# Gated feed-forward input projections from tile 5 on: one 512-column matmul over both parts of the residual in place of two of 256, with a second read-out and a written order on four engines

## The chip, the cores and the metric

The kernel runs on one core of a Trainium2 chip. The core has five engines that run side by side and meet only through semaphores: TensorE (PE in the rows below, with its weight loads shown apart as PEld), VectorE (DVE), ScalarE (ACT), GpSimd (POOL) and SyncE (SP), which here only issues transfers. TensorE reads both operands from SBUF and writes into PSUM, which has eight banks of 512 fp32 columns per partition. The metric is the device time of one execution in microseconds, the median of the runs.

## What is computed

A decoder trunk of two layers over 256 positions and 1,024 features, all in fp32: in each layer an attention block and then a gated feed-forward block with a short causal convolution. The change lies in the feed-forward block, which runs twice (D_FF is 2,816):

```python
def rmsnorm(x, g):
    y = xf * lax.rsqrt(jnp.mean(xf * xf, axis=-1, keepdims=True) + EPS)
    return (y * g.astype(jnp.float32)).astype(x.dtype)
...
def conv_ffn(h, w_in, conv_w, conv_b, w_out):
    u, g = jnp.split(h @ w_in, 2, axis=-1)
    g = lax.conv_general_dilated(g, conv_w[:, None, :], window_strides=(1,),
                                 padding=[(CONV_WIDTH - 1, 0)], ...
                                 feature_group_count=D_FF) + conv_b
    return (jax.nn.gelu(g, approximate=False) * u) @ w_out
...
    h = h + conv_ffn(rmsnorm(h, ffn_norm[layer]), ffn_w_in[layer], ...)
```

## The kernel before

**Two-part operands.** To keep fp32 accuracy with matmuls on a rounded type, each operand is held as a rounded part and the exact rest: weights as `whi` and `wlo`, the residual (times its norm gain, transposed, features on the partitions) as `xh` and `xl`, the activations of the feed-forward block as the two halves of a tile `o`. A product is three matmuls: high by high, high by rest, rest by high. `xh` and `xl` are each eight blocks (`KD`) of 128 features by 256 positions.

**Weights.** `PLAN` lists the weights in chunks of 128 x 2,048 in the order of use. SP loads a chunk into `raw` (three buffers), ACT copies it to `whi` (L144), DVE subtracts to get `wlo` (L145), each in two pieces of 1,024 columns; there are four buffer pairs. `need(name)` loads up to three chunks ahead and splits up to two ahead.

**A feed-forward tile.** The block runs over 22 tiles `f` of 128 of the 2,816 inner features. `dense(f)` multiplies all 256 positions with the tile's two weight blocks, u and g, into the two halves of one PSUM bank `pd`: 2 x 8 x 3 = 48 matmuls of 256 columns, by `colmajor`. `gate(f)` then multiplies the bank by the norm factor into `gbuf` (DVE, L743), runs the convolution (ACT L749, DVE L751 and L752), gelu (ACT L754), the product with u (POOL L755) and the split into `o` (ACT L757, DVE L758). Four tiles later (`LAGF`) `proj(f)` adds the tile's part of the output projection to accumulators `acc`, which keep their banks for the whole block: four banks and 24 matmuls of 256 columns for each tile in the first layer; five banks and 15 matmuls (nine of 512 columns, six of 256) in the second, whose output comes out positions first. In the second layer four sets of transposes (`phn`) bring the residual into that form; they stand behind tiles 6 to 9.

**Order.** TensorE takes its instructions in the order in which the program writes them. The order on the other engines is found by a scheduler, except at the start of the program. After tile 21, `proj` runs for the four tiles left over; in the second layer bank by bank (`TAIL`), for each bank tiles 18 to 21, and each finished bank is normalised and stored while the next one is summed.

Of the kernel before, what the change touches and what calls it, by code (L numbers as in the profile page):

```python
# [21 lines left out]
F32 = mybir.dt.float32  # L22
F32R = mybir.dt.float32r
AF = mybir.ActivationFunctionType
ALU = mybir.AluOpType
# [22 lines left out]
FIRST = 4  # L48
POOLSHARE = 3
TAIL = ((0, 0, 512), (0, 512, 1024), (1, 0, 512), (1, 512, 768), (1, 768, 1024))  # L50

# [49 lines left out]
def trunk(ctx, tc, x, rel_bias, small, lam_p, wpack, fin_g, onehot, addrow, tab, out):  # L101
# [21 lines left out]
    def pair(a):  # L123
        return a.rearrange("p (a b) -> p a b", a=2)

# [1 line left out]
    chunks, raws, splits = {}, {}, {}  # L127
# [44 lines left out]

# [1 line left out]
    iot = consts.tile([128, 128], F32)  # L174
# [8 lines left out]
    sel = consts.tile([128, 128], F32)  # L183
# [1 line left out]
    scr = consts.tile([128, 1], F32)  # L185
# [17 lines left out]

# [1 line left out]
    xh = xpool.tile([128, KD, S], F32R, name="xh")  # L205
    xl = xpool.tile([128, KD, S], F32R, name="xl")
    sqs = {}
# [57 lines left out]

# [1 line left out]
    def passmajor(items, ks):  # L267
# [23 lines left out]

# [1 line left out]
    Tt = consts.tile([128, 12, S], F32)  # L293
# [17 lines left out]

# [1 line left out]
    BLK = ((0, 256), (256, 384))  # L313
# [136 lines left out]

# [1 line left out]
    def proj_tile(acc, o, w, kk, first, last):  # L452
# [15 lines left out]

# [1 line left out]
    def interleave(env, units, tasks, store, first=0):  # L470
# [19 lines left out]
    def bc2(t):  # L490
        return t[:, None, :].to_broadcast([128, 2, S])
# [239 lines left out]

# [1 line left out]
    gbuf = [consts.tile([128, 2, S + 2], F32, name=f"gbuf{i}") for i in range(3)]  # L733
# [3 lines left out]
    def ffn(l, final):  # L737
        env, acts, box = {}, {}, {}
        cc = ccol[l]

        def gate(f, p):
            gb = gbuf[f % 3]
            nc.vector.tensor_tensor(gb[:, :, 2:], pair(p), bc2(env['r_bc']), op=ALU.mult)  # L743
            u, g = gb[:, 0], gb[:, 1]

            def col(i):
                return cc[:, i * NF + f:i * NF + f + 1]
            t1 = work.tile([128, S], F32, name="t1", tag="sc")
            nc.scalar.activation(t1, g[:, 2:], AF.Identity, bias=col(3), scale=col(2))  # L749
            t3 = work.tile([128, S], F32, name="t3", tag="pt", bufs=6)  # L750
            nc.vector.scalar_tensor_tensor(t3, g[:, 1:S + 1], col(1), t1, op0=ALU.mult, op1=ALU.add)  # L751
            nc.vector.scalar_tensor_tensor(t3, g[:, 0:S], col(0), t3, op0=ALU.mult, op1=ALU.add)  # L752
            ge = work.tile([128, S], F32, name="ge", tag="ex", bufs=6)
            nc.scalar.activation(ge, t3, AF.Gelu)  # L754
            nc.gpsimd.tensor_tensor(ge, ge, u[:, 2:], op=ALU.mult)  # L755
            o = t2("o", F32R)
            nc.scalar.activation(o[:, 0], ge, AF.Copy)  # L757
            nc.vector.tensor_tensor(o[:, 1], ge, o[:, 0].bitcast(F32), op=ALU.subtract)  # L758
            acts[f] = (o[:, 0], o[:, 1])

        def ug_items(p, f):
# [4 lines left out]
        def dense(f):  # L766
            p = bank("pd")
            colmajor(ug_items(p, f))
            gate(f, p)

        def proj(f):
            w = need(f"f{l}o{f // 2}")
            first, last = f == 0, f == NF - 1
            if first:
                box['acc'] = [bank("acc") for _ in range(len(TAIL) if final else 4)]
            if not final:
                proj_tile(box['acc'], acts[f], w, f % 2, first, last)
                return
            for i in range(len(TAIL)):
                proj_tail(f, i)  # L780

        def proj_tail(f, i):
            w = need(f"f{l}o{f // 2}")
            (oh, ol), (hi, lo) = acts[f], w
            tb, c0, c1 = TAIL[i]
            a = box['acc'][i][:, :c1 - c0]
            s = slice(tb * 128, (tb + 1) * 128)
            mm(a, oh[:, s], hi[:, f % 2, c0:c1], f == 0, False)
            mm(a, ol[:, s], hi[:, f % 2, c0:c1], False, False)
            mm(a, oh[:, s], lo[:, f % 2, c0:c1], False, f == NF - 1)  # L790
# [15 lines left out]
        hn = []  # L806
        for f in range(3, NF):
            dense(f)
            if f >= LAGF:
                proj(f - LAGF)  # L810
            if final and f >= 6 and len(hn) < 4:
                i = len(hn)
                p = bank("phn")
                for k in range(4):
                    kk = (i % 2) * 4 + k
                    nc.tensor.transpose(p[:, k * 128:(k + 1) * 128],
                                        hT[:, kk, (i // 2) * 128:(i // 2 + 1) * 128], ident)
                t = t2("hn", shape=(128, 512))
                nc.scalar.activation(t, p, AF.Copy)
                hn.append(t)  # L820
        if not final:
# [36 lines left out]

    # =================== program ===================
    warm = bank("warm")  # L860
# [114 lines left out]
```

## Time and profile before

| | us |
|---|---|
| median of 3 runs (lowest, highest) | 610.53 (610.17, 610.88) |
| profiled execution, first to last instruction (span) | 608.3 |
| TensorE busy in the span | 594.7 |
| VectorE, ScalarE, GpSimd busy | 410.6, 332.3, 116.0 |

The 2.2 us between the median and the span lie outside the first and last instruction of the profile. A matmul is pipelined: a row gives its own length, which overlaps the next one; the pace of a stretch is its length divided by its number of matmuls. Busy time of the other engines is an average over stages; whether an engine is late in a stage is seen from who waits there.

### The profile page before, as it was taken

The numbers are of one execution on the slowest core, as the hardware profiler recorded it, in microseconds if no ns is written. First come the engines' busy times: TensorE is split into PE (matmuls) and PEld (weight loads), VectorE is DVE, ScalarE is ACT, GpSimd is POOL, SyncE is SP. The second block draws the span as 40 slices with busy tenths as digits, with TensorE's granted clock in tenths as the row PEclk, the third lists the DMA queues.
The fourth block names the chain that finished last, engine by engine and source line by source line (L and its number), as shares of the span: only waits on it lengthen the run. The fifth ranks groups of instructions, "written<-read, shape, count | busy, mean of one in ns | idle before, by whom it ended". The sixth has DMA issues, their size and how long they took to land.

```text
span 608.3 us, 11226 instructions
## 1 busy us (share of the span) xinstructions
PE 594.7 (98%) x4622; PEld 571.0 (94%) x4622; DVE 410.6 (67%) x710; ACT 332.3 (55%) x579; POOL 116.0 (19%) x97
## 2 busy tenths in 40 slices
PE   8898999999999999999999999999999999999995
PEld 7887989999999999999999998999999999999994
DVE  5688767679765566656677884658976557665644
ACT  6458557566554445554564664646655445554433
POOL 4701022041201111111153111004120111111100
PEclk9999999999999999999999999999999999999998
DMA  8998544435545554554435333344554554455201
GB/s 278 334 333 297 201 152 142 154 124 208 185 167 204 208 201 157 197 204 156 159 141 208 138 140 140 139 157 155 208 197 155 204 208 175 173 206 184 94 2 70
DMA packets 19964, 108.83 MB, mean 179 GB/s; under 512 B 2430, under 2 KB 5448, under 8 KB 7752
## 3 DMA queue, kind: packets, MB, share of 16 engines
q1 hardware_dynamic: 16416, 104.17, 46.4%
q10 hardware_dynamic: 3336, 3.41, 1.8%
q8 instruction: 36, 0.59, 0.4%
q0 software_dynamic: 160, 0.52, 0.3%
q14 instruction: 16, 0.13, 0.1%
HBM read 107.02 MB, written 1.08 MB: 178 GB/s over the span
## 4 chain that ended last, share of the span: by engine, by line
PE 88%; DMA 4%; DVE 4%; issue 1%; ACT 1%; POOL 1%; SPq 0%; POOLq 0%; DVEq 0%; ACTq 0%
PE pd L121 50%; PE acc L121 27%; DMA raw<-in_wpack_dram 4%; PE pv L121 4%; DVE wlo L145 2%; PE pO L121 2%; PE pS L121 2%; PE puq L121 1%; DVE ex L340 1%; DVE sc L330 1%; PE pukv L121 0%; PE pT L344 0%; ACT whi L144 0%; ACT sqt L218 0%; PE pss L121 0%
## 5 line engine op out<-in xcount | busy, mean ns | idle before, releaser
L144 ACT ACTIVATE whi<-raw 128x1024 fp32r<-128x1024 f32 (+1 forms) x195 | 196.9, 1035 | 131.0 <-PE pd L121 70.3
L121 PE MATMUL pd<-xh,whi 128*128 128x256 f32 x928 | 260.7, 286 | 1.6 <-ACT whi L144 1.3
L121 PE MATMUL pd<-xh,wlo 128*128 128x256 f32 x928 | 258.0, 283 | 0.4 <-DVE wlo L145 0.4
L121 PE MATMUL pd<-xl,whi 128*128 128x256 f32 x928 | 257.8, 283 | 0.0
L145 DVE TENSOR_TENSOR wlo<-raw,whi 128x1024 fp32r<-128x1024 f32 (+1 forms) x183 | 222.5, 1234 | 36.4 <-ACT whi L144 36.2
L121 PEld LDWEIGHTS pd<-xh,whi 128*128 128x128 f32 x928 | 175.6, 191 | 3.4 <-ACT whi L144 1.7
L121 PEld LDWEIGHTS pd<-xh,wlo 128*128 128x128 f32 x928 | 175.7, 192 | 0.8 <-DVE wlo L145 0.8
L121 PEld LDWEIGHTS pd<-xl,whi 128*128 128x128 f32 x928 | 175.7, 192 | 0.1
L121 PE MATMUL acc<-o,whi 128*128 128x256 f32 x608 | 108.7, 280 | 0.0
L755 POOL TENSOR_TENSOR ge<-ge,gbuf 128x256 f32<-128x256 f32 x44 | 50.1, 1141 | 285.2 <-ACT ge L754 285.2
L121 PEld LDWEIGHTS acc<-o,whi 128*128 128x128 f32 x608 | 93.1, 188 | 0.3 <-issue 0.2
L121 PE MATMUL acc<-o,wlo 128*128 128x256 f32 x304 | 85.2, 280 | 0.0
L743 DVE TENSOR_TENSOR gbuf<-pd,r_bc 128x512 f32<-128x512 f32 x44 | 30.0, 690 | 50.7 <-PE pd L121 50.7
L121 PE MATMUL acc<-whi,o 128*128 128x512 f32 (+1 forms) x220 | 57.8, 349 | 0.0
L121 PEld LDWEIGHTS acc<-o,wlo 128*128 128x128 f32 x304 | 57.1, 188 | 0.0
L758 DVE TENSOR_TENSOR o<-ge,o 128x256 fp32r<-128x256 f32 x44 | 19.2, 444 | 49.9 <-ACT o L757 49.9
L757 ACT ACTIVATE o<-ge 128x256 fp32r<-128x256 f32 x44 | 18.4, 418 | 50.9 <-POOL ge L755 50.9
L145 POOL TENSOR_TENSOR wlo<-raw,whi 128x1024 fp32r<-128x1024 f32 (+1 forms) x12 | 26.5, 2206 | 102.6 <-ACT whi L144 56.0
L121 PEld LDWEIGHTS acc<-whi,o 128*128 128x128 f32 x220 | 38.2, 188 | 5.8
L121 PE MATMUL acc<-wlo,o 128*128 128x512 f32 (+1 forms) x110 | 38.3, 348 | 0.0
L754 ACT ACTIVATE ge<-t 128x256 f32<-128x256 f32 x44 | 17.8, 410 | 34.8 <-DVE t L752 34.8
L333 ACT ACTIVATE ex<-sc,nm 128x256 f32<-128x256 f32 (+1 forms) x56 | 24.8, 445 | 10.1 <-DVE nm L330 8.3
(153 smaller groups left out, 553.6 us busy)
## 6 DMA issues: line engine op xcount, KB each, us to landing
raw<-in_wpack_dram SPq DMA_DIRECT2D x95, 1024.0 KB, 4.8
raw<-in_wpack_dram SPq DMA_DIRECT2D x8, 256.0 KB, 4.5
Tt<-btab ACTq DMA_DIRECT2D x2, 1024.0 KB, 9.9
hT<-in_x_dram SPq DMA_DIRECT2D x4, 256.0 KB, 4.8
Tt<-btab ACTq DMA_DIRECT2D x1, 512.0 KB
raw<-in_wpack_dram SPq DMA_DIRECT2D x1, 512.0 KB
fin<-in_fin_g_dram POOLq DMA_DIRECT2D x2, 256.0 KB, 3.7
out_dram<-y SPq DMA_DIRECT2D x2, 256.0 KB, 3.1
```

Source lines behind the costliest of these rows:

```text
L121: nc.tensor.matmul(o, l, r, start=start, stop=stop, skip_group_check=True)
L144: nc.scalar.activation(hi[:, s], raw[:, s], AF.Copy)
L145: (eng or nc.vector).tensor_tensor(lo[:, s], raw[:, s], hi[:, s].bitcast(F32), op=ALU.subtract)
L330: nc.vector.tensor_tensor_reduce(out=t[:, a:b], in0=p[:, a:b], in1=rev(T, b - a), scale=-1.0, scalar=BIG, op0=ALU.add, op1=ALU.min, accum_ ...
L333: nc.scalar.activation(e[:, a:b], t[:, a:b], AF.Exp, bias=nm[:, i:i + 1], scale=-1.0, accum_out=den[:, i:i + 1])
L340: nc.vector.tensor_scalar(e[:, a:b], e[:, a:b], rd[:, i:i + 1], None, op0=ALU.mult)
L743: nc.vector.tensor_tensor(gb[:, :, 2:], pair(p), bc2(env['r_bc']), op=ALU.mult)
L754: nc.scalar.activation(ge, t3, AF.Gelu)
L755: nc.gpsimd.tensor_tensor(ge, ge, u[:, 2:], op=ALU.mult)
L757: nc.scalar.activation(o[:, 0], ge, AF.Copy)
L758: nc.vector.tensor_tensor(o[:, 1], ge, o[:, 0].bitcast(F32), op=ALU.subtract)
```

## The change

`xh` and `xl` become the two halves of each block of one tile `xs`, so that the 512 columns of a block's both parts lie side by side. Tiles 0 to 4 are as before. From tile 5 (`NARROW`) to 21, in both layers, u and g get a PSUM bank each. In each block a matmul of 512 columns takes `whi` over both parts of the residual, its two results standing in the two halves of the bank, and one of 256 columns adds `wlo` times the high part to the lower half. The halves must then be added: ACT copies the upper half to SBUF (`lowp`), DVE adds the lower half to it (`ug`), for u and g, and the product with the norm factor reads `ug`. In these tiles the orders of ACT, DVE, POOL and SP are those of the program text too, with the weight splits placed by hand among the steps of the gate; gelu and the split of tile f-1 stand inside tile f. The transposes of the second layer move to tiles 3 and 4, two sets each.

```diff
-    xh = xpool.tile([128, KD, S], F32R, name="xh")
-    xl = xpool.tile([128, KD, S], F32R, name="xl")
+    xs = xpool.tile([128, KD, 2, S], F32R, name="xs")
+    xh, xl = xs[:, :, 0], xs[:, :, 1]
...
+        def weights(f):
+            n = f"f{l}o{f // 2}"
+            return need(n) if f < NARROW - LAGF or f >= NF - LAGF else chunks[n]
+
         def proj(f):
-            w = need(f"f{l}o{f // 2}")
+            w = weights(f)
...
-        for f in range(3, NF):
+        for f in range(3, NARROW):
             dense(f)
+            if final:
+                hn_tile()
+                hn_tile()
             if f >= LAGF:
                 proj(f - LAGF)
-            if final and f >= 6 and len(hn) < 4:
...
+        def next_chunk():
+            i = split_at[0]
+            if i >= len(PLAN):
+                return [lambda: None] * 2
+            split_at[0] += 1
+            ps = pieces(i)[1]
+
+            def step(n):
+                if n == 0:
+                    open_split(i)
+                if n < len(ps):
+                    split_piece(i, ps[n])
+                if n == 1:
+                    load_next()
+            return [lambda: step(0), lambda: step(1)]
+
+        def product(f, i, p):
+            hi, lo = chunks[f"f{l}i{f}"]
+            for k in range(KD):
+                mm(p, hi[:, 8 * i + k], xs[:, k], k == 0, False)
+                mm(p[:, :S], lo[:, 8 * i + k], xs[:, k, 0], False, k == KD - 1)
+
+        def read_out(t, i, p):
+            lowp = work.tile([128, S], F32, name="lowp", tag="ex", bufs=6)
+            nc.scalar.activation(lowp, p[:, S:], AF.Copy)
+            nc.vector.tensor_tensor(t[:, i], p[:, :S], lowp, op=ALU.add)
+
+        need(f"f{l}i{NARROW}")
+        with tc.manual_schedule(engines={mybir.EngineType.Activation, mybir.EngineType.DVE,
+                                         mybir.EngineType.Pool, mybir.EngineType.SP}):
+            t3 = None
+            for f in range(NARROW, NF):
+                even = f % 2 == 0
+                pu, pg = bank("pd"), bank("pd")
+                product(f, 0, pu)
+                product(f, 1, pg)
+                if even:
+                    c = next_chunk()
+                    c[0]()
+                if t3 is not None:
+                    ge = gelu(f - 1, t3)
+                if even:
+                    c[1]()
+                if t3 is not None:
+                    act_split(f - 1, ge)
+                ug = t2("ug")
+                read_out(ug, 0, pu)
+                read_out(ug, 1, pg)
+                nc.vector.tensor_tensor(gbuf[f % 3][:, :, 2:], ug, bc2(env['r_bc']), op=ALU.mult)
+                c = next_chunk()
+                c[0]()
+                t3 = taps(f, conv(f))
+                c[1]()
+                proj(f - LAGF)
+            act_split(NF - 1, gelu(NF - 1, t3))
```

`conv`, `taps`, `gelu` and `act_split` are the steps of the former `gate`, cut apart and otherwise as they were.

On TensorE, in the first layer, the end of one tile's projection and the start of the next tile before:

```order
L121 MATMUL acc<-o,wlo 128x256
L121 MATMUL pd<-xh,whi 128x256
L121 MATMUL pd<-xl,whi 128x256
L121 MATMUL pd<-xh,wlo 128x256
L121 MATMUL pd<-xh,whi 128x256
L121 MATMUL pd<-xl,whi 128x256
L121 MATMUL pd<-xh,wlo 128x256
```

and the same kind of place now:

```order
L122 MATMUL pd<-xs,whi 128x512
L122 MATMUL pd<-xs,wlo 128x256
L122 MATMUL pd<-xs,whi 128x512
L122 MATMUL pd<-xs,wlo 128x256
L122 MATMUL pd<-xs,whi 128x512
```

Each pair of matmuls with the same `whi` block has become one of 512 columns, so 48 instructions for a tile are 32; the columns are as many as before.

On VectorE, one even and one odd tile in the middle of the first layer before (`t_` is the convolution):

```order
L743 TENSOR_TENSOR gbuf_125<-pd,r_bc 128x2x256
L145 TENSOR_TENSOR wlo<-raw,whi 128x1024
L751 SCALAR_TENSOR_TENSOR t_2571<-gbuf_125,ccol_309,t_2569 128x256
L145 TENSOR_TENSOR wlo<-raw,whi 128x1024
L752 SCALAR_TENSOR_TENSOR t_2571<-gbuf_125,ccol_309,t_2571 128x256
L145 TENSOR_TENSOR wlo<-raw,whi 128x1024 x2
L758 TENSOR_TENSOR o<-ge,o 128x256
L743 TENSOR_TENSOR gbuf_123<-pd,r_bc 128x2x256
```

and now, from the last step of an odd tile over an even one to the read-out of the next:

```order
L146 TENSOR_TENSOR wlo<-raw,whi 128x1024 x3
L767 TENSOR_TENSOR o<-ge,o 128x256
L877 TENSOR_TENSOR ug<-pd,lowp 128x256 x2
L900 TENSOR_TENSOR gbuf_122<-ug,r_bc 128x2x256
L146 TENSOR_TENSOR wlo<-raw,whi 128x1024
L754 SCALAR_TENSOR_TENSOR t_2617<-gbuf_122,ccol_308,t_2615 128x256
L755 SCALAR_TENSOR_TENSOR t_2617<-gbuf_122,ccol_308,t_2617 128x256
L146 TENSOR_TENSOR wlo<-raw,whi 128x1024
L767 TENSOR_TENSOR o<-ge,o 128x256
L877 TENSOR_TENSOR ug<-pd,lowp 128x256 x2
```

The read-out of a tile stands behind two weight splits and the activation split of the tile before in even tiles, and behind the activation split alone in odd ones.

On ScalarE, the last two tiles of the second layer before (`fsq` belongs to the final norm):

```order
L749 ACTIVATE t_6674<-gbuf_125,ccol_310 128x256
L144 ACTIVATE whi<-raw 128x1024
L754 ACTIVATE ge<-t_6676 128x256
L757 ACTIVATE o<-ge 128x256
L749 ACTIVATE t_6764<-gbuf_123,ccol_310 128x256
L754 ACTIVATE ge<-t_6766 128x256
L757 ACTIVATE o<-ge 128x256
L839 ACTIVATE fsq,fss_6794<-hn 128x512 x2
```

and now:

```order
L748 ACTIVATE t_6426<-gbuf_124,ccol_309 128x256
L145 ACTIVATE whi<-raw 128x1024
L760 ACTIVATE ge<-t_6428 128x256
L766 ACTIVATE o<-ge 128x256
L876 ACTIVATE lowp<-pd 128x256 x2
L748 ACTIVATE t_6496<-gbuf_122,ccol_309 128x256
L760 ACTIVATE ge<-t_6498 128x256
L766 ACTIVATE o<-ge 128x256
L925 ACTIVATE fsq,fss_6527<-hn 128x512 x2
```

Two copies have come between the last product and the last tile's gate.

## Rows read from the trace of the kernel before

**Rows 1.** The page: span, and busy time of each engine with its instructions.

```profile
span 608.3 us, 11226 instructions
PE 594.7 (98%) x4622; PEld 571.0 (94%) x4622; DVE 410.6 (67%) x710; ACT 332.3 (55%) x579; POOL 116.0 (19%) x97
```

**Rows 2.** The page: chain that ended last, share of span by line.

```profile
PE pd L121 50%; PE acc L121 27%; DMA raw<-in_wpack_dram 4%; PE pv L121 4%; DVE wlo L145 2%; PE pO L121 2%; PE pS L121 2%; PE puq L121 1%; DVE ex L340 1%; DVE sc L330 1%; PE pukv L121 0%; PE pT L344 0%; ACT whi L144 0%; ACT sqt L218 0%; PE pss L121 0%
```

**Rows 3.** Busy us by engine, tiles 7 to 21, layer one; then clock, DMA share.

```profile
171.69:297.65 125.96, 125.96 (x1058) 125.96 (x1058) 77.48 (x101) 60.89 (x87) 17.16 (x15) 1.00 0.50 184
```

**Rows 4.** Waits of PE in the whole span, from the longest: total, times, longest.

```profile
PE pT L344 <- DVE rd L335: 1.4, 1, 1.4
PE pd L121 <- ACT whi L144: 1.3, 2, 0.7
```

**Rows 5.** The chain in order of time: start, length, what, number of instructions.

```profile
82.70 5.47 PE pv L121 x24
...
151.68 2.83 PE acc L121 x24
154.51 5.75 PE pd L121 x48
...
297.65 14.14 PE acc L121 x120
...
501.79 2.79 PE acc L121 x15
...
587.19 8.40 PE acc L121 x39
```

**Rows 6.** Groups by line and shape: busy us, mean ns, idle before, releaser.

```profile
L144 ACT ACTIVATE whi<-raw 128x1024 fp32r<-128x1024 f32 x187 | 191.8, 1052 | 129.5 <-PE pd L121 70.3 <-issue 22.7 <-PE acc L121 17.8
L145 DVE TENSOR_TENSOR wlo<-raw,whi 128x1024 fp32r<-128x1024 f32 x179 | 219.7, 1246 | 36.3 <-ACT whi L144 36.2
L743 DVE TENSOR_TENSOR gbuf<-pd,r_bc 128x512 f32<-128x512 f32 x44 | 30.0, 690 | 50.7 <-PE pd L121 50.7
L749 ACT ACTIVATE t<-gbuf,ccol 128x256 f32<-128x256 f32 x44 | 25.9, 590 | 5.4 <-DVE gbuf L743 5.4
L752 DVE SCALAR_TENSOR_TENSOR t<-gbuf,ccol,t 128x256 f32<-128x256 f32 x44 | 21.7, 497 | 0.1
L751 DVE SCALAR_TENSOR_TENSOR t<-gbuf,ccol,t 128x256 f32<-128x256 f32 x44 | 20.9, 479 | 0.7 <-ACT t L749 0.7
L758 DVE TENSOR_TENSOR o<-ge,o 128x256 fp32r<-128x256 f32 x44 | 19.2, 444 | 49.9 <-ACT o L757 49.9
L757 ACT ACTIVATE o<-ge 128x256 fp32r<-128x256 f32 x44 | 18.4, 418 | 50.9 <-POOL ge L755 50.9
L754 ACT ACTIVATE ge<-t 128x256 f32<-128x256 f32 x44 | 17.8, 410 | 34.8 <-DVE t L752 34.8
L360 DVE TENSOR_TENSOR o<-pO,o 128x256 fp32r<-128x256 f32 x12 | 4.9, 420 | 7.7 <-ACT o L359 7.7
L359 ACT ACTIVATE o<-pO 128x256 fp32r<-128x256 f32 x12 | 4.5, 385 | 6.3 <-PE pO L121 6.3
```

**Rows 7.** The page: issues of weight loads, KB each, us to landing.

```profile
raw<-in_wpack_dram SPq DMA_DIRECT2D x95, 1024.0 KB, 4.8
```

**Rows 8.** Timeline of tiles 19 and 21 in the second layer, by engine.

```profile
575.28 1.81 POOL L755 TENSOR_TENSOR ge<-ge,gbuf 128x256 f32<-128x256 f32 x1 [8.26 <-ACT ge L754]
590.25 0.64 POOL L755 TENSOR_TENSOR ge<-ge,gbuf 128x256 f32<-128x256 f32 x1 [6.15 <-ACT ge L754]
...
587.23 0.69 DVE L743 TENSOR_TENSOR gbuf<-pd,r_bc 128x512 f32<-128x512 f32 x1 [2.22 <-PE pd L121]
...
591.38 0.42 DVE L758 TENSOR_TENSOR o<-ge,o 128x256 fp32r<-128x256 f32 x1 [1.72 <-ACT o L757]
...
590.93 0.42 ACT L757 ACTIVATE o<-ge 128x256 fp32r<-128x256 f32 x1 [0.82 <-POOL ge L755]
...
591.92 0.63 PE L121 MATMUL acc<-whi,o 128*128 128x512 f32 x2
```

More of the change, by code (lines that the diff above doesn't have):

```diff
@@ L49 @@
 POOLSHARE = 3
+NARROW = 5
 TAIL = ((0, 0, 512), (0, 512, 1024), (1, 0, 512), (1, 512, 768), (1, 768, 1024))
@@ L739, in ffn, with col, conv, taps @@
         cc = ccol[l]
[L741 to L747, printed above, removed]
+        def col(f, i):
+            return cc[:, i * NF + f:i * NF + f + 1]
+        def conv(f):
+            g = gbuf[f % 3][:, 1]
             t1 = work.tile([128, S], F32, name="t1", tag="sc")
-            nc.scalar.activation(t1, g[:, 2:], AF.Identity, bias=col(3), scale=col(2))
+            nc.scalar.activation(t1, g[:, 2:], AF.Identity, bias=col(f, 3), scale=col(f, 2))
+            return t1
+        def taps(f, t1):
+            g = gbuf[f % 3][:, 1]
             t3 = work.tile([128, S], F32, name="t3", tag="pt", bufs=6)
-            nc.vector.scalar_tensor_tensor(t3, g[:, 1:S + 1], col(1), t1, op0=ALU.mult, op1=ALU.add)
-            nc.vector.scalar_tensor_tensor(t3, g[:, 0:S], col(0), t3, op0=ALU.mult, op1=ALU.add)
+            nc.vector.scalar_tensor_tensor(t3, g[:, 1:S + 1], col(f, 1), t1, op0=ALU.mult, op1=ALU.add)
+            nc.vector.scalar_tensor_tensor(t3, g[:, 0:S], col(f, 0), t3, op0=ALU.mult, op1=ALU.add)
+            return t3
+        def gelu(f, t3):
             ge = work.tile([128, S], F32, name="ge", tag="ex", bufs=6)
             nc.scalar.activation(ge, t3, AF.Gelu)
-            nc.gpsimd.tensor_tensor(ge, ge, u[:, 2:], op=ALU.mult)
+            nc.gpsimd.tensor_tensor(ge, ge, gbuf[f % 3][:, 0, 2:], op=ALU.mult)
+            return ge
+        def act_split(f, ge):
             o = t2("o", F32R)
@@ L759, in gate @@
             acts[f] = (o[:, 0], o[:, 1])
+        def gate(f, p):
+            nc.vector.tensor_tensor(gbuf[f % 3][:, :, 2:], pair(p), bc2(env['r_bc']), op=ALU.mult)
+            act_split(f, gelu(f, taps(f, conv(f))))
         def ug_items(p, f):
@@ L782, in proj_tail @@
         def proj_tail(f, i):
-            w = need(f"f{l}o{f // 2}")
+            w = weights(f)
             (oh, ol), (hi, lo) = acts[f], w
@@ L806, in ffn, with hn_tile @@
         hn = []
-        for f in range(3, NF):
+        def hn_tile():
+            i = len(hn)
+            p = bank("phn")
+            for k in range(4):
+                kk = (i % 2) * 4 + k
+                nc.tensor.transpose(p[:, k * 128:(k + 1) * 128],
+                                    hT[:, kk, (i // 2) * 128:(i // 2 + 1) * 128], ident)
+            t = t2("hn", shape=(128, 512))
+            nc.scalar.activation(t, p, AF.Copy)
+            hn.append(t)
+        for f in range(3, NARROW):
@@ L808, in ffn, with load_next @@
             dense(f)
+            if final:
+                hn_tile()
+                hn_tile()
             if f >= LAGF:
                 proj(f - LAGF)
-            if final and f >= 6 and len(hn) < 4:
[L812 to L820, printed above, removed]
+        def load_next():
+            while raw_at[0] < min(split_at[0] + 3, len(PLAN)):
+                load_raw(raw_at[0])
+                raw_at[0] += 1
```

## The prediction

> **What bounds the kernel now.** The page comes first: TensorE is busy for 594.7 of 608.3 us, and no other engine for more than 410.6 [rows 1]. Busy time alone proves little, since it is a mean over stages, so the chain that ended last is next: half of it is the matmuls into `pd`, another 27% those into `acc` [rows 2]. Both together are the feed-forward blocks and some projections. Then the stage itself, by windows: from tile 7 to tile 21 of the first layer TensorE works for 125.96 of 125.96 us at full clock, VectorE for 77.48, ScalarE for 60.89, GpSimd for 17.16, the transfers half of the time [rows 3]. In the whole span TensorE's two longest waits are 1.4 and 1.3 us, and the one of `pd` (1.3 us in two waits) is all that an end to such waits could return there [rows 4]. So in the changed tiles nothing is waited for: the time of a tile is the time of its matmuls, and what the change is worth is read from their pace.
>
> In order of time the chain shows the pace. A tile's input product takes 5.75 us for 48 matmuls of 256 columns, 119.8 ns each. The first layer's `proj` takes 2.83 us for 24, 117.9 ns each. For 512 columns there are two stages: `pv` of the attention, 5.47 us for 24, 227.9 ns each, and the second layer's `proj`, 2.79 us for nine of 512 and six of 256; with 117.9 ns for the six, 231.4 ns remain for each of the nine [rows 5]. A matmul of 512 columns costs less than two of 256 in all of them, though only by 4 to 12 ns.
>
> **The matmuls: the term that carries the sum.** A tile had 48 matmuls of 256 columns, 12,288 columns; it gets 16 of 512 and 16 of 256, the same 12,288. What is saved is therefore only what a matmul costs beyond its columns, for 16 instructions a tile, and there are 17 tiles (5 to 21) in each of two layers, 34 in all, 544 pairs. No row has a residual block of 512 columns as the moving operand, so the cost is bounded from the nearest rows:
> - cheap end: 227.9 and 117.9 ns, 16 times their sum is 5.533 us a tile, 0.217 less than 5.75, 7.4 us over 34 tiles;
> - dear end: 231.4 and 119.8 ns, 5.619 us, 0.131 less, 4.4 us.
>
> I take the middle, 229.7 and 118.9 ns, 5.576 us a tile, 0.174 less: 5.9 us. Neither end is nearer: `pv` is a stage of 512 columns alone, the second layer's `proj` mixes both widths as the new tiles do, but with the activations as the stationary operand. A gain of nothing is not excluded; it is the first rival.
>
> **The read-out and the written order: hidden work.** Added to each tile are two copies of 128 x 256 out of PSUM on ScalarE (0.385 us each by `o<-pO`) and two adds from PSUM on VectorE (0.420 us by `o<-pO,o`); the product with the norm factor stays at 0.69 us [rows 6]. That is 0.77 us on ScalarE and 0.84 on VectorE, beside matmuls. Does it fit? An odd tile splits one weight chunk, an even one two. VectorE in an even tile: four pieces at 1.246, the activation split 0.444, two adds 0.84, the product 0.69, two convolution steps 0.976, in all 7.93 us; in an odd one, with two pieces, 5.44. A tile now lasts 5.58 + 2.83 = 8.41 us, a pair 16.8, against 13.4 us of VectorE. ScalarE has 6.40 and 4.29 us, from the same rows. The pair fits, the even tile narrowly.
>
> Since the orders are fixed, I laid one pair out by hand with these durations. In an even tile that begins at 0, VectorE ends the odd tile's last split at 2.2, the next two splits at 4.7, the activation split at 5.1, and frees the u bank at 5.5 and the g bank at 6.4. The first layer has four banks beside the accumulators, the second three; there the next tile's g product takes the freed u bank, at 8.4 + 2.8 = 11.2, which leaves 5.6 us. The last split of an odd tile ends 2.2 us behind the tile, and its chunk is for the tile after the next: 6.2 us left. With GpSimd's long product of 1.81 us [rows 8] in place of a short one these times hardly move, because the activation split still waits for VectorE's own queue. In the odd tile VectorE catches up while it waits for the end of the g product, so lateness isn't carried on. Loads keep their order on SP; three chunks are wanted in 16.8 us, and one lands 4.8 us after its issue [rows 7]. I count all this as nothing; if the cover went, the price is that of the third rival.
>
> **Seams.** Before tile 5 in the second layer, `pd` of tile 4, two `phn` and five accumulators fill the eight banks; the read-outs have the 2.79 us of the first `proj` to free one. The transposes cost TensorE the same in tiles 3 and 4 as in 6 to 9. At the first layer's end the last activations are wanted behind four `proj` (five run in 14.14 us there [rows 5]), 11.3 us after the last product, far more than the gate takes. The output of the whole kernel has no such cover. In the second layer the last tile's product ends at 587.19; GpSimd's product, the copy and the rest follow until 591.35 and 591.80, and TensorE wants the copy at 591.92 and the rest one matmul (0.23) later [rows 5, 8]. So there is 0.57 us to spare for the copy and 0.35 for the rest. A copy and an add, 0.385 + 0.420, and two hand-offs of some 0.04 (587.23 against 587.19) now stand ahead of that chain: 0.88 us more. TensorE waits 0.31 for the copy and 0.22 more for the rest, together 0.5 us. The bounds are 0.3, if the rest's wait vanishes, and 1.7, if GpSimd takes 1.81 instead of 0.64 us there [rows 8].
>
> **Sum.** 608.3 - 5.9 + 0.5 = 602.9 us of span. The profile's span is 2.2 us under the runs' median of 610.53; with that kept, 605.1 us. Its own bounds: 610.5 - 7.4 + 0.3 = 603.4 and 610.5 - 4.4 + 1.7 = 607.8.
>
> **Rivals.**
> *Columns alone set the pace.* If a 512-column pass over the residual takes 2 x 119.8 = 239.6 ns, the merge returns nothing, and the tail's 0.5 us is left: 611.0 us; in part of the way, 608 to 611. For it: the columns are equal, and the nine of 512 in `proj` are at 231.4 against 2 x 117.9 = 235.8, nearly in proportion [rows 5]. Against it: `pv` at 227.9, and no row reaches 239.6. The Trainium skill, TensorE: Matmul & The Clock Gate, Back-to-back issue gap, gives a warm matmul N/2.4 + 2.5 ns, so that merging would save only 2.5 ns a pair: an estimate of 1.4 us, 609.6 us with the tail. The rows don't agree with its figures (119.8 and 227.9 for its 109.2 and 215.8), but they don't exclude so small a fixed part.
>
> *Weight loads set the pace.* The loads are busy for 125.96 of 125.96 us, like the matmuls [rows 3]; a load hidden behind 512 columns could leave the 256 columns behind it at their bare time. From 227.9 and 119.8 ns, a column is 0.4223 ns and the fixed part 11.7; without it the `wlo` matmul takes 108.1 ns, a tile 16 x (227.9 + 108.1) = 5.376 us, 0.374 less, 12.7 us in all: 598.3 us. Against it: if the six of 256 in the second layer's `proj` took 108.1, its nine would take 237.9, which `pv` denies. The Trainium skill, Perfetto Trace Analysis, Identifying the Most-Contended Engine, has the loads' busy share as the measure of TensorE's headroom, which would speak for this one.
>
> *VectorE becomes the bound: slower.* The place is the even tile, 7.93 of 8.41 us. In the written order a read-out cannot pass a split that waits for its copy. If a pair's VectorE time with the waits in its queue passed 16.8 us, that is 3.4 us above the sum of its rows or 26% longer instructions, the excess would be paid in each of 17 pairs: 1 us each makes 605.1 + 17 = 622 us, and from 0.32 us a pair the change loses. Against it: 77.48 of 125.96 us busy today [rows 3], and splits that wait for ScalarE only 36.3 us in the whole span [rows 6].
>
> **How the numbers follow.** Forecast, 603.4 to 607.8: 0.57. Columns alone, 607.8 to 611: 0.17. Loads, under 603.4: 0.11. VectorE, over 611: 0.10. Left for a seam or something unseen: 0.05, more than half of it slower. 0.2% is 1.2 us, about what a measurement here can tell from no change: faster means under 609.3. The forecast, the loads and 0.07 of the columns' case lie there: 0.75; same 0.12; slower 0.13. The range takes in the forecast, the columns' case and the near part of the loads' case: 601.5 to 611.0.
>
> **What the changed profile would show.** Input products of 32 matmuls in 5.5 to 5.65 us, back to back with `proj`; a tile in about 8.4 us (8.58 before); PE without waits of `pd` on a bank, `ug` or `wlo`; adds of `ug` in even tiles some 2.7 us behind the u product; and a first wait of TensorE near the end, on the activation copy and rest of tile 21, of about half a microsecond. A product of 5.75 us is the first rival, one under 5.45 the second, and PE rows that wait for VectorE in every second tile the third. I would be wrong altogether if the pace of the `wlo` matmuls changed with the new layout of `xs`, for which no row stands.

## The result and the profile after

| | before | after |
|---|---|---|
| median (lowest, highest), 4 runs each, us | 610.42 (610.17, 610.88) | 606.85 (604.95, 607.95) |
| ratio of the times, 95% interval | | 0.9939 [0.9916, 0.9962] |
| span of the profiled execution, us | 608.3 | 606.1 |

The change is 0.6% faster, 3.6 us. The profiled execution, 607.95 us, is the longest of the four of after, 1.1 us above their median.

The page of after, span, busy time and chain, against [rows 1, 2]:

```profile
span 606.1 us, 10380 instructions
PE 591.7 (98%) x4078; PEld 544.6 (90%) x4078; DVE 443.0 (73%) x778; ACT 351.6 (58%) x647; POOL 103.0 (17%) x97
PE pd L122 48%; PE acc L122 26%; PE pv L122 4%; DMA raw<-in_wpack_dram 3%; DVE wlo L146 3%; PE pO L122 2%; PE pS L122 2%; DMA hT<-in_x_dram 1%; PE puq L122 1%; DVE ex L341 1%; DVE sc L331 1%; ACT whi L145 1%; PE pukv L122 0%; POOL ge L761 0%; PE pT L345 0%
```

There are 544 matmuls and 544 weight loads fewer, and TensorE still bounds the kernel: its busy time fell by 3.0 us while that of VectorE rose by 32. The share of the loads fell from 94% to 90%.

The chain of after in order of time (start, length, what, number of instructions), against [rows 5]:

```profile
154.94 5.65 PE pd L122 x32
...
171.78 5.55 PE pd L122 x32
177.34 2.83 PE acc L122 x24
...
294.66 14.13 PE acc L122 x120
...
446.72 4.40 PE pd L122 x16
451.12 3.00 PE acc L122 x15
454.12 5.56 PE pd L122 x32
...
579.62 5.57 PE pd L122 x32
...
590.30 4.00 PE acc L122 x15
```

A tile's product is 5.55 us in the first layer and 5.56 in the second, where it was 5.75. The one row that stands out is at 446.72: of tile 5 in the second layer only the last 16 matmuls are on the chain, and they take 4.40 us, not 2.78 (half of 5.56). The windows of after, tiles 7 to 21 of the first layer, against [rows 3], and the stretch behind that row (busy us by engine, then clock, DMA share):

```profile
171.78:294.66 122.88, 122.88 (x819) 112.96 (x818) 91.54 (x131) 69.68 (x116) 12.75 (x15) 1.00 0.53 189
447.00:452.00 5.00, 5.00 (x20) 4.22 (x20) 0.79 (x2) 1.22 (x4) 0.00 (x0) 0.66 0.25 100
```

Fifteen products and fourteen `proj` take 122.88 us instead of 125.96, all of it TensorE's work, at full clock; the weight loads now have 9.9 us to spare there. In the second stretch the granted clock is 0.66. TensorE's longest waits, against [rows 4]:

```profile
PE pd L122 <- ACT hn L833: 2.2, 1, 2.2
...
PE acc L122 <- ACT o L766: 0.2, 1, 0.2
```

Neither was there before; those between them are as before, within half a microsecond or so. The groups that the read-out adds, against [rows 6]:

```profile
L877 DVE TENSOR_TENSOR ug<-pd,lowp 128x256 f32<-128x256 f32 x68 | 28.5, 419 | 52.7 <-ACT lowp L876 52.7
L876 ACT ACTIVATE lowp<-pd 128x256 f32<-128x256 f32 x68 | 25.9, 381 | 81.2 <-PE pd L122 81.1
```

They last what the nearest rows of before had given, 419 and 381 ns for 420 and 385. The timeline at both places of the waits, with tile 10 of the first layer ahead of them, its first matmul for g and its add of u (start, length, engine; in brackets the idle time before, and what ended it):

```profile
199.54 0.39 PE L122 MATMUL pd<-xs,whi 128*128 128x512 f32 x1
...
201.93 0.41 DVE L877 TENSOR_TENSOR ug<-pd,lowp 128x256 f32<-128x256 f32 x1
...
441.62 0.40 PE L122 MATMUL pd<-xs,whi 128*128 128x512 f32 x1
...
441.97 0.39 PE L122 MATMUL pd<-xs,whi 128*128 128x512 f32 x1
...
444.28 0.28 PE L122 MATMUL pd<-xs,wlo 128*128 128x256 f32 x1
446.72 0.50 PE L122 MATMUL pd<-xs,whi 128*128 128x512 f32 x1 [2.16 <-ACT hn L833]
...
448.36 0.63 PE L122 MATMUL pd<-xs,whi 128*128 128x512 f32 x1
...
449.00 0.63 PE L122 MATMUL pd<-xs,whi 128*128 128x512 f32 x1
...
453.95 0.40 PE L122 MATMUL pd<-xs,whi 128*128 128x512 f32 x1
...
444.61 0.42 ACT L760 ACTIVATE ge<-t 128x256 f32<-128x256 f32 x1 [1.79 <-DVE t L755]
445.77 0.42 ACT L766 ACTIVATE o<-ge 128x256 fp32r<-128x256 f32 x1 [0.75 <-POOL ge L761]
446.09 1.07 ACT L833 ACTIVATE hn<-phn 128x512 f32<-128x512 f32 x2
...
585.27 0.38 ACT L876 ACTIVATE lowp<-pd 128x256 f32<-128x256 f32 x1 [2.39 <-PE pd L122]
...
589.84 0.42 ACT L766 ACTIVATE o<-ge 128x256 fp32r<-128x256 f32 x1 [0.81 <-POOL ge L761]
...
590.30 0.96 PE L122 MATMUL acc<-whi,o 128*128 128x512 f32 x2 [0.23 <-ACT o L766]
```

In tile 5 of the second layer the product of u runs (441.62 to 444.28), and that of g cannot begin: it wants a second bank, and besides the five accumulators and u's bank there are only two, which still hold transposes. Their copy `hn` on ScalarE (446.09) stands behind gelu and split of tile 4, and gelu waited 1.79 us for VectorE. Behind the wait a pair of matmuls, one of 512 and one of 256 columns, comes to take 0.64 us (448.36 to 449.00) where 0.35 is usual (441.62 to 441.97): the granted clock is at the lower of its two levels, 1.2 GHz. From the first matmul of tile 5 to the first of tile 6 there are 12.33 us (441.62 to 453.95).

Where the time went, from the two profiled executions. The chain of before in the second layer, beside [rows 5]:

```profile
443.05 5.75 PE pd L121 x48
...
451.59 5.75 PE pd L121 x48
...
460.13 0.44 PE phn L816 x4
```

Tiles 5 to 21 of the first layer, from the start of tile 5 to the end of the last product, take 139.72 us (154.94 to 294.66) instead of 143.14 (154.51 to 297.65): 3.42 less. Tiles 6 to 21 of the second layer take 131.07 (454.12 to 585.19) instead of 133.84 (451.59 to 587.19, less four sets of transposes of 0.44): 2.77 less. With 0.17 of the matmuls of tile 5 and its `proj` (8.37 us without the stop, as transposes back shows below, for 8.54) that is 6.4 us. The stop at tile 5 gives back some 4, the 39 matmuls behind the last product 0.7 (585.19 to 594.30, 9.11 us, instead of 8.40). 608.3 - 6.4 + 4.0 + 0.7 = 606.6, against a span of 606.1. The half microsecond that is left lies outside the changed tiles: tile 5 of the first layer begins 0.4 us later (154.94 for 154.51), and from the last of the 39 matmuls to the end of the span there are 0.9 us less (594.30 to 606.1, for 595.59 to 608.3).

### The profile page after: what moved, and what is told of

It reads as the page before. It is cut to its first block, busy times and chain, and to the rows that moved or that the text cites. A ratio compares the mean times of both kernels' runs of the same rounds, so it can differ in the third digit from the quotient of the medians.

```text
span 606.1 us, 10380 instructions
## 1 busy us (share of the span) xinstructions
PE 591.7 (98%) x4078; PEld 544.6 (90%) x4078; DVE 443.0 (73%) x778; ACT 351.6 (58%) x647; POOL 103.0 (17%) x97
## 4 chain that ended last, share of the span: by engine, by line
PE 84%; DVE 6%; DMA 4%; ACT 2%; issue 1%; POOL 1%; SPq 0%; POOLq 0%; ACTq 0%; DVEq 0%
PE pd L122 48%; PE acc L122 26%; PE pv L122 4%; DMA raw<-in_wpack_dram 3%; DVE wlo L146 3%; PE pO L122 2%; PE pS L122 2%; DMA hT<-in_x_dram 1%; PE puq L122 1%; DVE ex L341 1%; DVE sc L331 1%; ACT whi L145 1%; PE pukv L122 0%; POOL ge L761 0%; PE pT L345 0%
## 5 line engine op out<-in xcount | busy, mean ns | idle before, releaser
L122 PE MATMUL pd<-xs,whi 128*128 128x256 f32 (+1 forms) x1312 | 331.3, 332 | 3.7 <-ACT hn L833 2.2
L122 PE MATMUL pd<-xs,wlo 128*128 128x256 f32 x928 | 258.0, 283 | 0.4 <-DVE wlo L146 0.4
L146 DVE TENSOR_TENSOR wlo<-raw,whi 128x1024 fp32r<-128x1024 f32 (+1 forms) x183 | 229.3, 1278 | 26.4 <-ACT whi L145 26.2
L122 PEld LDWEIGHTS pd<-xs,whi 128*128 128x128 f32 x1312 | 221.0, 191 | 27.1 <-ACT whi L145 2.5
L122 PEld LDWEIGHTS pd<-xs,wlo 128*128 128x128 f32 x928 | 175.7, 192 | 0.8 <-DVE wlo L146 0.8
L761 POOL TENSOR_TENSOR ge<-ge,gbuf 128x256 f32<-128x256 f32 x44 | 37.4, 851 | 294.8 <-ACT ge L760 294.8
L876 ACT ACTIVATE lowp<-pd 128x256 f32<-128x256 f32 x68 | 25.9, 381 | 81.2 <-PE pd L122 81.1
L877 DVE TENSOR_TENSOR ug<-pd,lowp 128x256 f32<-128x256 f32 x68 | 28.5, 419 | 52.7 <-ACT lowp L876 52.7
L748 ACT ACTIVATE t<-gbuf,ccol 128x256 f32<-128x256 f32 x44 | 26.4, 601 | 12.0 <-DVE gbuf L900 10.1
L122 PE MATMUL pv<-whi,xs 128*128 128x512 f32 x96 | 30.2, 395 | 0.0
```

What stands on the lines that cost most here:

```text
L122: nc.tensor.matmul(o, l, r, start=start, stop=stop, skip_group_check=True)
L146: (eng or nc.vector).tensor_tensor(lo[:, s], raw[:, s], hi[:, s].bitcast(F32), op=ALU.subtract)
L748: nc.scalar.activation(t1, g[:, 2:], AF.Identity, bias=col(f, 3), scale=col(f, 2))
L761: nc.gpsimd.tensor_tensor(ge, ge, gbuf[f % 3][:, 0, 2:], op=ALU.mult)
L876: nc.scalar.activation(lowp, p[:, S:], AF.Copy)
L877: nc.vector.tensor_tensor(t[:, i], p[:, :S], lowp, op=ALU.add)
```

## The experiments

The theory: merging the matmuls returns some 6.4 us, and a stop for a PSUM bank in tile 5 of the second layer takes back a good half of it. The rivals: the stop is a chance of one execution, the gain comes from the layout of `xs` or the written order instead of the matmuls, or VectorE has been near to being the bound. Ratios are to the kernel before on the same chip.

| kernel | us, median | ratio [95%] |
|---|---|---|
| transposes back | 603.74 | 0.9894 [0.9871, 0.9916] |
| two of 256 | 613.96 | 1.0057 [1.0039, 1.0075] |
| scheduler's order | 607.1 | 0.9957 [0.9934, 0.9979] |
| layout alone | 610.08 | 1.0001 [0.9982, 1.002] |
| back, last tile the old way | 603.86 | 0.9906 [0.989, 0.9922] |
| back, grouped | 603.89 | 0.9914 [0.9895, 0.9933] |
| back, splits doubled in even tiles | 603.83 | 0.9909 [0.9887, 0.9931] |
| back, all splits doubled | 667.31, one run | |
| before, transposes early | 609.58 | 0.9989 [0.9977, 1.0002] |
| after again | 606.87 | 0.9946 [0.9929, 0.9962] |
| transposes back again | 603.92 | 0.9901 [0.9887, 0.9916] |

**Transposes back.** The change, but with the transposes of the second layer in tiles 6 to 9 as before the change, here between a tile's products and its `proj`.

```diff
         for f in range(3, NARROW):
             dense(f)
-            if final:
-                hn_tile()
-                hn_tile()
...
                 read_out(ug, 1, pg)
+                if final and 6 <= f < 10:
+                    hn_tile()
```

> The changed kernel with one edit: the four sets of transposes of the second layer stand in tiles 6 to 9 again, one set between a tile's products and its projection, on the third free bank. Theory, moved transposes: the changed kernel's one long wait of TensorE (2.2 us, tile 5 of the second layer, on a copy of hn) comes from two unread transpose banks, and the half clock of the matmuls behind it from that wait; both go, so tile 5's product falls from 9.3 us with the wait to 5.55, the span by some 3.7 us, to about 602.4, and the runs' median to 603 to 604 against 610.4 of the kernel before. Rival, two banks a tile: at the layer's start the read-outs are late whatever the transposes do, so that tile 5 still waits 1 us or more for a bank, and the span stays over 604.

Measured: 603.74 us. The chain at tile 5 of the second layer:

```profile
439.43 5.56 PE pd L122 x32
444.99 2.81 PE acc L122 x15
```

The tile and its `proj` take 8.37 us, 3.96 less than the 12.33 of after, TensorE has no wait for `hn`, and the granted clock is 1.00 from 436 to 457. The stop comes from where the transposes stand.

**Two matmuls of 256 columns.** Everything of the change but the merge.

```diff
-                mm(p, hi[:, 8 * i + k], xs[:, k], k == 0, False)
+                mm(p[:, :S], hi[:, 8 * i + k], xs[:, k, 0], k == 0, False)
+                mm(p[:, S:], hi[:, 8 * i + k], xs[:, k, 1], False, False)
```

> The changed kernel with the merge alone undone: the pass over both parts of the residual is two matmuls of 256 columns into the two halves of the bank; layout, banks, read-out and written order stay. Theory, merge: 48 matmuls at about 119.8 ns again, 5.75 us a tile instead of 5.55, 34 tiles, 6.8 us more than the changed kernel: about 613, slower than the kernel before by some 2.5 us (its seam and tail without its gain). Rival, layout: the faster pace comes from the new place of the two parts beside each other, and 48 matmuls take 5.6 us or less (116.7 ns each), about 608.

Measured: 613.96 us, 4.2 us slower than before on that chip (609.81), where some 2.5 were expected. Its longest wait of TensorE, a product in the chain, and the window of the 5 us around the end of that wait:

```profile
PE pd L122 <- ACT hn L833: 2.1, 1, 2.1
```

```profile
180.58 5.75 PE pd L122 x48
```

```profile
447.00:452.00 5.00, 2.91 (x24) 2.71 (x24) 1.74 (x4) 2.08 (x5) 0.64 (x1) 1.00 0.58 213
```

The product is back at 5.75 us and the stop is still there, though the granted clock stays at 1.00: without the merge the rest of the change only costs. Against the scheduler's order, 607.1 us on the same chip with merge and stop, the medians are 6.9 us apart. The two spans are 4.7 apart (610.8 and 606.1), as the lower clock came behind the stop there and not here. With the 1.8 us that this clock cost in the execution of after (12.33 - 8.37 - 2.16), that makes 6.5.

**The scheduler's order.** The change without the written order.

```diff
-        with tc.manual_schedule(engines={mybir.EngineType.Activation, mybir.EngineType.DVE,
-                                         mybir.EngineType.Pool, mybir.EngineType.SP}):
+        if True:
```

> The changed kernel without the written order in tiles 5 to 21: the scheduler orders ACT, DVE, POOL and SP as elsewhere. If the written order only has to keep the read-outs in time, and VectorE has 3.4 us to spare in a pair of tiles, the scheduler's order does as well: product 5.55 us a tile, no wait of PE in tiles 6 to 21, within 2 us of the changed kernel. Rival, the order carries the change: read-outs or splits come late, PE waits in many tiles, 5 us or more above the changed kernel.

Measured: 607.1 us. The window of tiles 7 to 20, first layer:

```profile
171.78:289.10 117.32, 117.32 (x786) 108.08 (x785) 85.78 (x125) 68.20 (x112) 8.94 (x14) 1.00 0.52 189
```

Fourteen tiles take 117.32 us, 8.38 each, as in after (171.78 to 289.10 there too). The stop is here as well (2.2 us), and the two ratios overlap: no effect of the written order can be seen.

**Layout alone.** The kernel before with `xh` and `xl` as halves of `xs`.

```diff
-    xh = xpool.tile([128, KD, S], F32R, name="xh")
-    xl = xpool.tile([128, KD, S], F32R, name="xl")
+    xs = xpool.tile([128, KD, 2, S], F32R, name="xs")
+    xh, xl = xs[:, :, 0], xs[:, :, 1]
```

> The kernel before with one edit: the two parts of the residual are the halves of one tile, block by block, as in the changed kernel; all matmuls stay at 256 columns. Theory, merge: the input product stays at 5.75 us for 48, the time at 610.4 within 0.2%. Rival, layout: the product falls to 5.6 us or less, the time by 5 us or more.

Measured: 610.08 us, no difference. The chain has the same product as before ("180.08 5.75 PE pd L121 x48"), so the layout does not change the pace.

**Transposes back, and the last tile the old way.** Tile 21 of the second layer takes 48 matmuls into one bank, and its product with the norm factor reads PSUM.

```diff
-                product(f, 0, pu)
-                product(f, 1, pg)
+                last = final and f == NF - 1
...
+                            mm(q, hi[:, m], xh[:, k], k == 0 and i == 0, False)
+                            mm(q, hi[:, m], xl[:, k], False, False)
+                            mm(q, lo[:, m], xh[:, k], False, k == KD - 1)
...
+                ug = pair(pu) if last else t2("ug")
```

> The kernel of e1 (transposes in tiles 6 to 9) with one more edit: the last tile of the second layer is computed as in the kernel before, 48 matmuls of 256 columns into one bank that VectorE reads directly, without copy and adds. Theory, read-out at the tail: the wait of TensorE for the activations of tile 21 (0.6 us between matmuls in e1's trace, and one at half clock or not behind it) goes; the tile costs 0.2 us more of matmuls; net 0.3 to 0.6 us below e1, about 603.3. Rival: the chain of the tail is set by something else (the gate's own length), and the time is 0.2 us above e1.

Measured: 603.86 us. Its chain at the end:

```profile
575.18 5.74 PE pd L122 x48
580.92 8.41 PE acc L122 x39
```

The 39 matmuls take 8.41 us again, so the 0.7 us at the end come from the read-out; the product costs 0.17 us more. The net of about half a microsecond that was expected doesn't show in the median, which is that of transposes back (603.74, on another chip).

**Grouped.** Transposes back, and in each product first the eight matmuls of 512 columns, then the eight of 256.

```diff
                 mm(p, hi[:, 8 * i + k], xs[:, k], k == 0, False)
+            for k in range(KD):
                 mm(p[:, :S], lo[:, 8 * i + k], xs[:, k, 0], False, k == KD - 1)
```

> The kernel of e1 with the matmuls of a product in another order: first the eight of 512 columns, then the eight of 256, no longer in turn. If a matmul costs what its width costs, a product stays at 5.55 us and the time at e1's 603.7. If the turn-taking helps the narrow ones (116 to 117 ns in the changed kernel against 119.8 before, because their loads are hidden behind 512 columns), the eight in a row go back to 119.8 and the wide ones to pv's 227.9, 5.56 us: no difference in sum, but a different split. Rival: wide ones in a row cost 235 to 240, 5.7 us or more, 5 us above e1.

Measured: 603.89 us. One product of g in the timeline:

```profile
189.98 2.00 PE L122 MATMUL pd<-xs,whi 128*128 128x512 f32 x8
191.82 1.12 PE L122 MATMUL pd<-xs,wlo 128*128 128x256 f32 x8
192.78 0.40 PE L122 MATMUL acc<-o,whi 128*128 128x256 f32 x2
```

Eight of 512 columns take 1.84 us, 230 ns each, eight of 256 take 0.96, 120 each; a tile's product is 5.59 us instead of 5.55. In alternation the 256-column matmul takes (5.55 / 16) - 0.230 = 0.117 us, if one of 512 takes 230 ns there too; the starts of the matmuls in tiles 7 to 20 of after bear that out (230.5 ns on average from one of 512 to the next, 116.7 from one of 256). The difference, 0.04 us a tile, 1.4 in all, is not seen in the medians.

**Splits doubled in even tiles.** Transposes back, and one more subtraction for each of the two pieces of the even tile's own chunk: 2.5 us more of VectorE for a pair of tiles, of the 3.4 that the prediction left it.

```diff
                     split_piece(i, ps[n])
+                    if twice:
+                        hi, lo, raw = splits[i], splits[i, 1], raws[i]
+                        nc.vector.tensor_tensor(lo[:, ps[n]], raw[:, ps[n]], hi[:, ps[n]].bitcast(F32),
+                                                op=ALU.subtract)
...
                 if even:
-                    c = next_chunk()
+                    c = next_chunk(True)
```

> The kernel of e1 with two more subtractions of 128 x 1,024 on VectorE in every even tile (the two of one weight chunk are done twice, same values): 2.5 us more in a pair of tiles, 15.9 us against 16.8 of TensorE. Theory, VectorE has 3.4 us to spare in a pair: no wait of PE in tiles 6 to 21, time within 1 us of e1's 603.7. Rival, the even tile is already at its limit (7.93 of 8.4 us): lateness shows, 10 us or more above e1.

Measured: 603.83 us, as without it. Tiles 7 to 20:

```profile
171.78:289.10 117.32, 117.32 (x787) 108.03 (x786) 105.32 (x142) 68.02 (x112) 11.77 (x14) 0.95 0.53 189
```

VectorE works for 105.32 of 117.32 us, and TensorE still waits for nothing in this stretch: the cover is real.

**All splits doubled.** The same in every split, 7.4 us a pair.

```diff
-                c = next_chunk()
+                c = next_chunk(True)
                 c[0]()
                 t3 = taps(f, conv(f))
```

> The kernel of e1 with every weight subtraction of VectorE in tiles 5 to 21 done twice: 7.4 us more in a pair of tiles, 20.8 us against 16.8. Theory, VectorE becomes the bound: 4 us a pair once the slack of 6 us is used up after some three pairs, so about 20 us in each layer, 640 to 650 us in all. Rival, the slack is larger than counted from the rows: under 615.

Measured: 667.31 us, one run. The window of 171.78 to 289.10, and TensorE's longest waits:

```profile
171.78:289.10 117.32, 108.22 (x691) 97.59 (x691) 115.31 (x141) 55.44 (x92) 10.92 (x12) 0.97 0.45 159
```

```profile
PE pd L122 <- DVE ug L878: 17.2, 7, 3.3
PE acc L122 <- ACT o L766: 13.1, 2, 10.4
PE pd L122 <- DVE wlo L863: 11.9, 8, 2.3
```

VectorE, at work for 115.31 of 117.32 us, is the bound now: its splits of one pair and those of the next start 20.3 us apart (209.73, 230.03, 250.32, 270.61), where 13.4 + 7.4 = 20.8 was to be expected. The kind of thing is as expected, the size is not: 17 pairs of 20.3 instead of 16.8 us are 60 us on top of 603.8, and some 4 more are not accounted for. The slack that was to spare the first three pairs of a layer only puts the lateness off: TensorE meets part of it at the end of the first layer's block, in one wait of 10.4 us for an activation.

**Before, with early transposes.** The kernel before, its transposes behind tiles 3 and 4, two sets each.

```diff
             dense(f)
-            if f >= LAGF:
-                proj(f - LAGF)
-            if final and f >= 6 and len(hn) < 4:
-                i = len(hn)
+            for i in range(len(hn), len(hn) + 2) if final and f < 5 else ():
...
+            if f >= LAGF:
+                proj(f - LAGF)
```

> The kernel before with one thing of the change: the transposes of the second layer stand behind tiles 3 and 4, two sets each, all products as before. If the stop at tile 5 comes from the early transposes alone, TensorE waits for the copy of hn here too, the product of tile 5 takes about 7.9 us, and the time is 612 to 614 us. If it takes both, the early transposes and a tile that wants two banks at once, a tile of one bank finds the bank of the tile before free, TensorE waits for no hn, and the time is that of before: 610 us, plus or minus 0.5.

Measured: 609.58 us, no difference from before. Its chain at tile 5 of the second layer:

```profile
440.15 0.87 PE phn L813 x8
441.02 2.79 PE acc L121 x15
443.82 5.74 PE pd L121 x48
```

No wait: a tile of one bank finds the bank of tile 4 free. It takes both, the early transposes and the second bank.

**After and transposes back, once more, on the same chip.** No edit.

> The changed kernel once more, unaltered, on the chip of the two runs beside it, to see how far the stop at tile 5 and the half clock behind it repeat. By the seam's theory 606 to 608 us, again a wait of about 2.2 us for hn, and 2 to 4 us above the run with the transposes back. If the stop were a chance of one execution, no such wait, and the two agree.

> The changed kernel with the transposes back behind the projections of tiles 6 to 9, once more, for a comparison on one chip with the changed kernel. By the seam's theory 603.5 to 604 us, 2 to 4 us less than the changed kernel. If only the wait itself counts, 2.2 us less at most; if the half clock behind it comes each time, 3.5 to 4 us less.

Measured: 606.87 us (five runs, 605.10 to 607.31) and 603.92 (four, 603.37 to 604.35): 2.95 apart, and the two do not overlap. After in this profile, first the timeline, then the window of the same 5 us:

```profile
440.51 0.40 PE L122 MATMUL pd<-xs,whi 128*128 128x512 f32 x1
...
445.62 0.54 PE L122 MATMUL pd<-xs,whi 128*128 128x512 f32 x1 [2.17 <-ACT hn L833]
...
452.88 0.40 PE L122 MATMUL pd<-xs,whi 128*128 128x512 f32 x1
```

```profile
447.00:452.00 5.00, 5.00 (x22) 4.16 (x21) 1.21 (x3) 1.39 (x3) 0.00 (x0) 0.76 0.05 18
```

The wait and the lower clock are here again, and tile 5 with its `proj` takes 12.37 us, 4.0 more than with the transposes back. The version with the transposes back beats both kernels. The stop is no chance, and it is worth about 3 us in the median: more than the wait alone (2.2), less than the 4.0 of the two profiled executions.

## Why the prediction was right, and where it failed

The forecast, 605.1 us, lies 1.7 us under the measured 606.85, and the time is inside the forecast's own bounds of 603.4 to 607.8. That is partly luck: one step failed, the runs put about 3 us on it in the median (the profiled executions 4), and the bounds happened to have room for that. The sum without that step comes nearest to the kernel with the transposes back: 0.9894 and 0.9901 of before, which is 604.0 and 604.4 us for the 610.42 here, 0.7 to 1.1 under the forecast.

**The matmuls.** Right in kind and under-sized. Instead of 5.9 us they return 6.4. In the first layer a product takes 5.55 us where 5.576 was taken: the 512 columns cost 230 ns, between the two bounds, and the 256 columns in alternation 117, just below the cheap end. In the second layer `proj` rose from 2.79 to 2.81 us, so that a tile gains 0.17 there and 0.2 in the first. For a pair of merged matmuls that is 12.6 ns (3.42 us over 17 x 16 pairs). The Trainium skill, TensorE: Matmul & The Clock Gate, Back-to-back issue gap, has a fixed part of 2.5 ns for a single warm matmul, by which merging would save only that. The measurement decides, and it is five times as much.

**The read-out and the written order.** The cost of nothing was right. The adds of tile 10 come where they had been laid out: the u add ends at 202.34, 2.8 us behind the u product (199.54, the start of the first matmul for g in the timeline), where 2.7 had been given; TensorE waits for no `ug`. The 3.4 us that VectorE was to have left are borne out from both sides, by 2.5 us more in a pair of tiles that cost nothing and by 7.4 that cost 3.5. The written order carries none of it, since the scheduler's does as well.

**Seams: the step that failed.** The prediction counted eight full banks before tile 5 and said that "the read-outs have the 2.79 us of the first `proj` to free one". One was freed, that of tile 4, and u's product ran on it. But by the change itself the tile wants two. The Trainium skill, PSUM — Partial Sum Buffer, The four PSUM rules, says that a matmul's output fits in one bank, at most 512 fp32 columns; the trace agrees, in that the 512-column product of g needed a bank apart from u's, and waited 2.16 us for it. The second bank hung on the copy of a transpose, and nothing had been asked of when ScalarE gets to that: behind gelu and split of tile 4, at 446.09. Transposes back shows the cause, early transposes alone that it takes both parts. What the step left out altogether is that TensorE would run on at the lower clock behind the wait.

The tail was right in kind, 0.7 us instead of 0.5: the copy arrives 5.1 us behind the product (585.19 to 590.26), as worked out (4.16 + 0.88), and the old way in the last tile takes it away.

**The rivals.** Columns alone would have left 239.6 ns for 512 columns; they take 230, and with the merge undone the gain is gone. Weight loads as the pace would have given 5.376 us a product; it is 5.55, with loads that are no longer busy all the time (112.96 of 122.88 us). The Trainium skill, Perfetto Trace Analysis, Identifying the Most-Contended Engine, names that share, beside the share of peak arithmetic, as the measure of TensorE's headroom. Here the share of the loads fell from 100% of the stretch to 92% and the time by 2.4%, with no wait in it. VectorE did not become the bound: 2.5 us more of it in a pair of tiles bring no wait. The layout of `xs`, named as what would make the prediction wrong altogether, changes nothing.

**What stays open.** Of the four profiled executions with a wait of some 2.2 us at tile 5, the clock fell in three and not in that with two matmuls of 256; why not there wasn't found. How often it falls in runs without a profile isn't known; all that they have is a mean granted clock. In the second series of after, four runs with 0.995 or 0.996 took 606.74 to 607.31 us and the fifth, with 0.998, took 605.10, as if the clock had fallen in four. But in the first series three runs with 0.999 took 604.95, 606.22 and 607.47. So the step from 4.0 us in the profiles to 2.95 in the medians is not explained.

## What to carry to other kernels

When a tile comes to need more PSUM banks, count at each seam not only how many banks are free but which instruction frees each, and what stands ahead of that instruction on its engine; here moving four transposes back made 606.87 us into 603.92. Merging two matmuls that share a stationary block paid little here, 12.6 ns of the 359 that the three matmuls of a block had taken, so that the wait of 2.16 us alone weighs as much as 170 merges. Where TensorE is the bound, small steps on other engines could be added without cost here, and doing one of them twice showed how much room was left.

## What the runs showed of the hardware

- Behind a wait of 2.16 us TensorE ran on at a granted clock of 0.66 in a stretch of 5 us (0.76 in the second execution, over the same 5 us, where the wait ended 1.1 us earlier), with pairs of 0.64 us instead of 0.35; tile 5 lost 1.8 us to that beside the wait itself (12.33 - 8.37 - 2.16). Read by single microseconds, the clock had still been at 1.00 in the wait and, of the first execution, from 447 to 448, when the matmuls had set in again; from 448 to 451 it was at 0.50 to 0.52. After a wait of 2.1 us in the kernel with two matmuls of 256 the clock stayed at 1.00.
- A matmul of 256 columns takes 120 ns in a row of its like and 117 between matmuls of 512; one of 512 takes 230 in both.
- With the splits doubled in even tiles the record gives a granted clock of 0.95 through the whole stretch, and yet fourteen tiles take the same 117.32 us as at 1.00. Such a record alone says little; the pace of the matmuls has to be looked at beside it.
